# Two mixer gates' first 512 columns: from two plain row products to one seven-product Strassen unit spread over the gate columns and u, with a smaller scratch for dynamic DMAs and more buffers

## The chip, the cores and the metric

One core of a Trainium2 chip runs the whole program. Its engines are TensorE (PE, with PEld for its weight loads), VectorE (DVE), ScalarE (ACT), GpSimd (POOL) and SyncE (SP), which here only issues transfers. The metric is the device time of one execution in microseconds; the median of the runs is given. All data are float32, and a matmul in float32r is used three times over for one float32 product (below).

## The reference, cut to what matters

A trunk of two layers on 256 tokens of width 1024. Each layer is a half-step feed-forward (SwiGLU, 2816 wide), a mixer, and a second half-step feed-forward, each followed by a layer normalisation.

```python
z = x @ w_in
u, v, q, k, val, gates = jnp.split(z, SPLITS, axis=-1)
...
g = jax.nn.sigmoid(gates.reshape(bsz, seq, N_BRANCH, D_MODEL) + gate_b)
m = g[:, :, 0] * (h_a @ w_branch[0]) + g[:, :, 1] * (h_b @ w_branch[1])
return m @ w_out
```

`h_a` is a spatial gating unit (u times a causal mix of the normalised v), `h_b` is differential attention (q, k, val, 8 heads). There are two gates of 1024 columns each, one per branch. The change is in how the first 512 columns of both gates are computed.

## The kernel before

**Three matmuls for one.** A float32 operand is split into a high part (`hi`, rounded to float32r, by ACT) and a low part (`lo`, the difference, by DVE). A product is hi·hi + lo·hi + hi·lo. For each MB of weights that SP fetches into a `raw` buffer (4 of them), `stream` makes two half-blocks of 128 x 1024: ACT line 195 writes `whi`, DVE line 197 writes `wlo`. There are 8 buffers of each. Both can run ahead of TensorE as far as these buffers reach.

**Two forms of product.** In the row form (`rows_b`, `three`, line 283) the tokens are stationary and 512 weight columns move: per block of 128 tokens and 128 rows of weights, three matmuls of 512 columns. In the column form (`gemm_a2`, lines 295 and 302) the weights are stationary: 8 matmuls of 512 moving columns per 128 output columns, which carry the tokens' hi and lo parts side by side, and 8 of 256 for the low weights. Its results are emptied from PSUM by a copy of ACT (`r`, line 303) and an addition of DVE (line 305 or 307). `gemm_a2` takes 1 MB of weights for 256 output columns.

**Order of the work.** TensorE runs in the order in which the program is written. The instructions of the other engines are put in order by a planner ahead of time, by priority (`step` raises it per MB fetched) and by when their data are ready in the planner's own account; on the chip each engine then runs its list in that fixed order and waits where a datum is late. Tasks that go beside the products (attention, normalisation, sums) are generators: `beside(task, delay)` puts one on a list, and `beat(w)`, called after each product with its length, starts the next step of each task whose time has come. One beat is about 2.7 us of TensorE. `with behind(ins)` queues an instruction after another one on the same engine.

**The mixer.** val (row form, `gemm_b2`); eight query/key products in column form with rotary (`rope`); meanwhile four `attend` tasks, one for each pair of heads, run their steps: scores on TensorE (line 1017), maxima on DVE, exponentials on ACT (1031), the difference of the two maps (1040), POOL's copies that part the halves of a word for the transposing DMA (line 216, `parted`), the DMA on SP (`moved`, line 220), ACT's copies that join them again (1065), the products with val (1071 and 1073), and the norm per head, with POOL's small instructions (lines 268 to 276). Then for each gate in turn: `gate_rows`, the first 512 columns in row form (48 matmuls; two fetches), and `gate_columns`, the other 512 in two column products. After both gates, two column products of u, two row products of v, the other two of u, and the branches.

`gate_rows` is a plain product with all four half-blocks held (`tail=TAIL`): 2 token blocks x 8 row blocks x 3. DVE adds the bias row and ACT takes the tanh (lines 1125 and 1126). Its results, `grow[br][t]`, are read much later, by `branch_rows`.

**Strassen's scheme in the feed-forward part.** `seven` and `gemm_seven` already use Winograd's seven products for two 512-column weight groups at a time. The input is cut into token blocks t and row halves, the weights into row halves and two column groups. The sums of the input are made once (`sums_of_x`, `strassen_sums`: four differences on DVE, in place, and four splits into stationary blocks `xhs`). The sums of the weights are made either by DVE (`plus`) or by an accumulating DMA issued from POOL (`gather`, line 353), which adds a second block from HBM to a raw buffer: two issues of 512 KB. A block can be added to only when the split of its old value is done. `product` (line 376) is 4 row blocks x 3 matmuls of 512 columns into a bank that several products may share.

**Memory.** PSUM has two pools of four banks, `bank()` and `side_bank()`. In SBUF, beside the weight buffers, there are 26 `slot` tiles, and two pools of small tiles: `main` (`t512`, 3 tiles) and `side` (`s512`, 4 tiles). The normalisation leaves its transposed output in two tiles of each (`norm.rows`). [...]

Of the kernel before, what the change touches and what calls it, by code (L numbers as in the profile page):

```python
# [11 lines left out]
F32 = mybir.dt.float32  # L12
# [33 lines left out]
RAW, HL = 4, 8  # L46
# [8 lines left out]
def trunk(ctx, tc, x, xT, w13a, w13b, w2, wb, wqk, wu, wg, wgr, wbr, wbrr, wo, gateb, gatebr, sgug, sgub, sguwT, sgubias, lam, diffg,  # L55
# [42 lines left out]
    def t512(s, n=3):  # L98
        return tmp.tile([P, 512], F32, tag="main", name=name(s), bufs=n)

    def s512(s, n=4):
        return tmp.tile([P, 512], F32, tag="side", name=name(s), bufs=n)
# [491 lines left out]
    class Norm:  # L594
# [36 lines left out]
        def kept(self):  # L631

            y = self.y[-1][:, D - self.group :]
            unit, v = (tmp.tile([P, 512], F32R, tag="main", name=name("kept"), bufs=3) for _ in range(2))
# [145 lines left out]

    def ffn(l, f, i, norm, last=False):
# [57 lines left out]
        def sums_of_h():  # L839

            h11, h21, h12, h22 = (held[v] for v in ((0, 0), (0, 1), (1, 0), (1, 1)))
            made = [[h_hi[1], h_lo[1]]] + [[slots("sum", 2, F32R)[0] for _ in range(2)] for _ in range(2)]
            made.append([tmp.tile([P, 512], F32R, tag="side", name=name("sum"), bufs=4) for _ in range(2)])
            yield from strassen_sums(sums, made, h11, h21, h12, h22, 1.5)

        def sums_of_x():
# [6 lines left out]
            def home(tag):  # L853
                pool, n = {"main": (tmp, 3), "side": (tmp, 4), "slot": (act, 26)}[tag]
# [4 lines left out]

        def strassen_sums(to, made, v11, v21, v12, v22, apart=1, after=lambda: None):  # L860
            to[:] = [tuple(lambda k, v=v: v[:, k * P : (k + 1) * P] for v in m) for m in made]
            for n, (out, a, b, op) in ((0, (v22, v21, v22, ALU.subtract)), (2, (v21, v11, v21, ALU.subtract)),
                                       (1, (v11, v22, v11, ALU.subtract)), (3, (v12, v12, v11, ALU.add))):
                with behind(after()):
                    V.tensor_tensor(out=out, in0=a, in1=b, op=op)
                if n in (2, 3):
                    yield apart
            for n, out in ((0, v22), (2, v21), (1, v11), (3, v12)):
                split(*(v if len(out.shape) == 2 else v.rearrange("p (k t) -> p k t", k=4) for v in made[n]), out)
                yield apart  # L870
# [98 lines left out]
    def mixer(l, i, norm):  # L969
# [33 lines left out]
        def attend(hp, qT, kT):  # L1003
# [17 lines left out]
            def exps(t, banks):  # L1021
                nk = (t + 1) * P
                pp = []
                for m in range(2):
                    o = m * 4 + t * 2
                    p = s512("pp", 4)[:, : 2 * nk]
# [82 lines left out]

        for hp in range(HEADS // 2):  # L1110
# [6 lines left out]
        gates, grow = [], []  # L1117

        def gate_rows(br):

            gr = [slots("gr", 2)[0] for _ in range(NT)]
            grow.append(gr)

            def done(t, ps, c, n):
                added[0] = V.tensor_tensor(out=gr[t], in0=ps, in1=gbias[:, br * 512 : (br + 1) * 512], op=ALU.add).ins
                emptied[0] = A.activation(gr[t], gr[t], AF.Tanh, scale=0.5).ins
# [12 lines left out]
        for br in range(2):  # L1139
            gate_rows(br)  # L1140
            gate_columns(br)
# [43 lines left out]
        def spatial(gp):  # L1185
# [7 lines left out]
            s1 = s512("sgu", 4)  # L1193
# [164 lines left out]
```

## Time and profile before

| | before |
|---|---|
| runs, median of 3 | 1186.83 us (1186.79 to 1187.02) |
| profiled execution: first to last instruction (its span; the page has no other time of it) | 1185.1 us |
| instructions | 16676 |
| TensorE busy, matmuls | 1180.5 us, 5777 |
| DVE, ACT, POOL busy | 1013.1, 828.1, 287.5 us |
| DMA issued from SP (q1), from POOL (q0) | 248.67 MB, 24.71 MB |
| mixer of layer 0: query/key, gates and first half of u | 202.3 to 250.3 us, 250.3 to 312.9 us |
| the same of layer 1 | 788.8 to 836.6 us, 836.6 to 899.3 us |

A row of a group reads: line, engine, operation, tiles out<-in, shapes, count, then busy us and the mean of one in ns, then the idle time before them with what ended it. A row of a line's own view gives the shortest, middle and longest duration in ns. A row of the timeline is start, duration, engine, line, operation; in square brackets the idle time before it. A row of transfers gives count, KB each and the median us from issue to landing. Matmuls overlap, so the mean of one (390 ns) is longer than their spacing. PE is TensorE.

### The profile page before, as it was taken

To read this page: it belongs to the slowest core of one execution; us is meant where nothing else is said; L and a number is where in the kernel's file an instruction comes from. 1 tells how busy PE (TensorE), PEld (TensorE's weight loads), DVE (VectorE), ACT (ScalarE), POOL (GpSimd) and SP (SyncE) were. 2 spreads that over 40 slices of the span, in tenths; PEclk is the share of its full clock that TensorE was granted. 3 is DMA by queue.
4 is the path that set the end of the run, shared out by engine and by line. 5 is a ranking of instruction groups with operands and counts; after the bars stand their busy time and mean duration, and the time that the engine had idled before them with its cause. 6 is when DMAs were issued, how large, how long until landed. Compare 5 with 4: busy or idle time off the path is not lost.

```text
span 1185.1 us, 16676 instructions
## 1 busy us (share of the span) xinstructions
PE 1180.5 (100%) x5777; PEld 995.0 (84%) x5777; DVE 1013.1 (85%) x1562; ACT 828.1 (70%) x1419; POOL 287.5 (24%) x350
## 2 busy tenths in 40 slices
PE   9999999999999999999999999999999999999998
PEld 8888888888888888888888888888888888888887
DVE  6989989788688989889899889888965989988895
ACT  6688658559955677876667876576788556679761
POOL 1011201247420220051020161003564112102600
PEclk9999999999999999999999999999999999999999
DMA  9869976767865658699668689586666755786881
GB/s 355 265 198 262 287 273 208 266 193 238 246 205 173 227 188 273 187 275 267 239 220 265 190 278 280 198 290 232 212 204 208 250 181 174 247 254 208 273 260 36
DMA packets 129621, 275.10 MB, mean 232 GB/s; under 512 B 89041, under 2 KB 90369, under 8 KB 105473
## 3 DMA queue, kind: packets, MB, share of 16 engines
q1 hardware_dynamic: 121968, 248.67, 63.5%
q0 software_dynamic: 6992, 24.71, 8.7%
q8 instruction: 45, 0.74, 0.2%
q10 hardware_dynamic: 576, 0.66, 0.2%
q14 instruction: 40, 0.32, 0.1%
HBM read 248.05 MB, written 1.05 MB: 210 GB/s over the span
## 4 chain that ended last, share of the span: by engine, by line
PE 99%; DVE 0%; DVEq 0%; issue 0%
PE bank L283 46%; PE bank L295 15%; PE sbank L376 12%; PE bank L410 10%; PE bank L302 8%; PE sbank L410 3%; PE bank L530 2%; PE sbank L1017 1%; PE bank L376 1%; PE sbank L1073 1%; PE sbank L1191 1%; PE sbank L542 0%; PE sbank L1071 0%; PE sbank L714 0%; DVE xtok L701 0%; DVE st L643 0%
## 5 line engine op out<-in xcount | busy, mean ns | idle before, releaser
L197 DVE TENSOR_TENSOR wlo<-raw,whi 128x1024 fp32r<-128x1024 f32 (+1 forms) x346 | 379.4, 1123 | 51.8 <-ACT whi L195 38.0
L195 ACT ACTIVATE whi<-raw 128x1024 fp32r<-128x1024 f32 (+1 forms) x350 | 323.4, 952 | 135.1 <-PE bank L283 43.0
L283 PE MATMUL bank<-whi,x 128*128 128x512 f32 x1224 | 386.4, 390 | 0.0
L283 PEld LDWEIGHTS bank<-whi,x 128*128 128x128 f32 x1224 | 229.8, 188 | 47.8
L283 PE MATMUL bank<-wlo,x 128*128 128x512 f32 x612 | 238.2, 389 | 0.0
L249 DVE TENSOR_TENSOR wlo<-raw,whi 128x1024 fp32r<-128x1024 f32 (+1 forms) x123 | 142.9, 1185 | 20.3 <-ACT whi L247 11.4
L247 ACT ACTIVATE whi<-raw 128x1024 fp32r<-128x1024 f32 (+1 forms) x123 | 121.1, 1003 | 51.2 <-DVE raw L359 23.9
L295 PE MATMUL bank<-x,whi 128*128 128x512 f32 x640 | 153.3, 391 | 0.0
L295 PEld LDWEIGHTS bank<-x,whi 128*128 128x128 f32 x640 | 118.2, 188 | 23.8
L283 PEld LDWEIGHTS bank<-wlo,x 128*128 128x128 f32 x612 | 114.9, 188 | 23.1
L229 POOL COPY seven<-seven 128x512 uint16<-128x512 uint16 x16 | 58.8, 3733 | 135.2 <-ACT whi L195 54.6
L302 PEld LDWEIGHTS bank<-x,wlo 128*128 128x128 f32 x640 | 81.4, 191 | 2.9
L302 PE MATMUL bank<-x,wlo 128*128 128x256 f32 x640 | 82.6, 283 | 0.0
L410 PE MATMUL bank<-whi,hhi 128*128 128x512 f32 (+1 forms) x182 | 68.2, 374 | 0.0
L410 PE MATMUL bank<-whi,hlo 128*128 128x512 f32 (+1 forms) x182 | 67.9, 373 | 0.0
L410 PE MATMUL bank<-wlo,hhi 128*128 128x512 f32 (+1 forms) x182 | 67.9, 373 | 0.0
L993 POOL TENSOR_TENSOR swap<-swap,sin_t 128x512 f32<-128x512 f32 x16 | 26.9, 1680 | 101.2 <-DMA swap<-z 84.4
L757 POOL COPY nvia<-ntwo 128x256 uint16<-128x256 uint16 x20 | 10.0, 547 | 161.2 <-DMA ntwo<-nvia 148.2
L303 ACT ACTIVATE r<-bank 128x256 f32<-128x256 f32 x96 | 34.9, 373 | 16.3 <-PE bank L302 16.1
L376 PE MATMUL sbank<-whi,xhs 128*128 128x512 f32 x128 | 42.0, 389 | 0.0
L410 PEld LDWEIGHTS bank<-whi,hlo 128*128 128x128 f32 x182 | 34.3, 188 | 6.0
L410 PEld LDWEIGHTS bank<-whi,hhi 128*128 128x128 f32 x182 | 34.3, 188 | 6.0
(292 smaller groups left out, 2157.6 us busy)
## 6 DMA issues: line engine op xcount, KB each, us to landing
raw<-in_w13b SPq DMA_DIRECT2D x68, 1024.0 KB, 6.0
raw<-in_w SPq DMA_DIRECT2D x32, 1024.0 KB, 7.0
raw<-in_wb SPq DMA_DIRECT2D x16, 1024.0 KB, 6.7
raw<-in_wqk SPq DMA_DIRECT2D x16, 1024.0 KB, 6.2
home<-in_w13b SPq DMA_DIRECT2D x16, 512.0 KB, 5.9
raw<-in_w13a SPq DMA_DIRECT2D x8, 1024.0 KB, 4.9
home<-in_w SPq DMA_DIRECT2D x16, 512.0 KB, 4.9
raw<-in_wgr SPq DMA_DIRECT2D x8, 1024.0 KB, 5.4
```

The costliest lines, as they stand in the source:

```text
L195: inline(A, A.activation(h, r, AF.Copy).ins)
L197: low = eng.tensor_tensor(out=w, in0=r, in1=h.bitcast(F32), op=ALU.subtract).ins
L229: eng.tensor_copy(out=o, in_=i)
L247: a = A.activation(hi, src, AF.Copy).ins
L249: return a, eng.tensor_tensor(out=lo, in0=src, in1=hi.bitcast(F32), op=ALU.subtract).ins
L283: PE.matmul(ps, xx, w, start=start and n == 0, stop=stop and n == 2)
L295: PE.matmul(b[-1], hi[:, k * P : (k + 1) * P], xc(k), start=k == 0, stop=False)
L302: PE.matmul(b[n][:, :T], lo[:, k * P : (k + 1) * P], xc(k)[:, :T], start=False, stop=k == KT - 1)
L303: emptied[0] = A.activation(r[:, s], b[n][:, T:], AF.Copy, scale=scale).ins
L376: PE.matmul(ps, x[o](k), y, start=start and k == n == 0, stop=stop and k == 3 and n == 2, skip_group_check=True)
L410: PE.matmul(q[c][t][:, :n] if o == 0 else more[:, :n], x(k, t), y, start=k == 8 and m == 0 and (c, t) != (1, 0) and not o, stop=k == FT - ...
L993: turned_by[0] = G.tensor_tensor(out=s3, in0=s3, in1=s, op=ALU.mult).ins
```

## The change

In each mixer, `gate_rows` and its two plain products are gone. `gates_by_rows` computes the first 512 columns of both gates as one Strassen unit: the two gates are the two column groups, the two token blocks the two row groups. It is a generator with seven products; `next(products)` stands before each of the four gate-column products, before the first two products of u, and after the second. It fetches three blocks of weights (the first gate's two halves and the second gate's second), and adds to two of them four times by `gather`, one beat after the product that used the old value. The first bank is held through all seven products, another through the third and fourth. Sums go into the four tiles `g00` to `g11` in DVE additions; the four tanh are as before.

`sums_of_x` in the mixer starts 3.5 beats into the query/key products, with 0.7 beats between its steps, and takes eight `slot` tiles. `strassen_sums` is moved out of `ffn` unchanged, so that both can call it.

There are 5 raw buffers instead of 4, 4 `main` tiles instead of 3 and 5 `side` tiles instead of 4 (12 KB per partition more); the scratch for dynamic DMAs falls from 16384 to 4096 bytes per partition, 12 KB less.

```diff
-RAW, HL = 4, 8
+RAW, HL = 5, 8
+MAIN, SIDE = 4, 5
...
+        gates, grow, x_sums = [], [], []
+
+        def sums_of_x():
+            made = [slots("xhs", 4, F32R) for _ in range(4)]
+            t11, t12, t21, t22 = (norm.rows[v] for v in ((0, 0), (0, 1), (1, 0), (1, 1)))
+            yield from strassen_sums(x_sums, made, t11, t21, t12, t22, 0.7, lambda: added[0])
+
+        def gates_by_rows():
+
+            x11, x12, x22 = (tuple(lambda k, o=o, t=t, h=h: x_cat[h][:, k, o + t * P : o + (t + 1) * P] for o in (0, T))
+                             for t, h in ((0, 0), (0, 1), (1, 1)))
+            (w11, w21), (w12, w22) = ([wgr[l, br, 0][:, o : o + CH] for o in (0, CH)] for br in range(2))
+            grow.extend([slots("gr", 2)[0] for _ in range(NT)] for _ in range(2))
+            (g00, g10), (g01, g11) = grow
+
+            def add_in(raw, w):
+                def task():
+                    gather(raw, w)
+                    yield 0
+                beside(task(), 1)
+            bias = [gbias[:, br * 512 : (br + 1) * 512] for br in range(2)]
+
+            def sum_up(out, in0, in1, op, end=False):
+                added[0] = V.tensor_tensor(out=out, in0=in0, in1=in1, op=op).ins
+                if end:
+                    emptied[0] = A.activation(out, out, AF.Tanh, scale=0.5).ins
+
+            bx = bank()
+            r1 = fetch(w11)
+            product(bx, x11, pieces(r1), True, False)
+            add_in(r1, w12)
+            sum_up(g00, bx, bias[0], ALU.add)
+            yield
+            bq = bank()
+            product(bq, x12, pieces(fetch(w21)), True, True)
+            sum_up(g00, bq, g00, ALU.add, True)
+            yield
+            bz = bank()
+            product(bz, x_sums[0], pieces(r1), True, False)
+            add_in(r1, w22)
+            sum_up(g11, bz, bias[1], ALU.add)
+            yield
+            r3 = fetch(w22)
+            product(bz, x_sums[3], pieces(r3), False, True)
+            add_in(r3, w12)
+            sum_up(g01, bz, bias[1], ALU.add)
+            yield
+            product(bx, x_sums[1], pieces(r1), False, False)
+            add_in(r1, w21)
+            sum_up(g01, g01, bx, ALU.subtract, True)
+            yield
+            product(bx, x_sums[2], pieces(r3), False, False)
+            sum_up(g11, g11, bx, ALU.subtract, True)
+            yield
+            product(bx, x22, pieces(r1), False, True)
+            sum_up(g10, bx, bias[0], ALU.add, True)
+            yield
+
+        beside(sums_of_x(), 3.5)
...
-        gates, grow = [], []
-
-        def gate_rows(br):
...
-            gemm_b(wgr[l, br, 0], KT, xh, xl, done, tail=TAIL)
+        products = gates_by_rows()
 
         def gate_columns(br):
             gt = slots("gate", KT // 2)
             gates.append(gt)
             for c in range(KT // 4):
+                next(products)
                 (_, b), = gemm_a2([wg[l, br, c]], both, lambda m: t512("gz"), lambda: t512("r"))
...
         for br in range(2):
-            gate_rows(br)
             gate_columns(br)
...
             for gp in gps:
+                if gp < 2:
+                    next(products)
                 uu = slots("u", 2)[0]
...
+            if gp == 1:
+                next(products)
...
-    nc = bacc.Bacc("TRN2", target_bir_lowering=False, num_devices=1)
+    nc = bacc.Bacc("TRN2", target_bir_lowering=False, num_devices=1, dynamic_dma_scratch_size=4096)
```

More of the change, by code (lines that the diff above doesn't have):

```diff
@@ L96, in parts, with t512, s512 @@
         return (lambda k: f(k)[:, :T]), (lambda k: f(k)[:, T:])
[L98 to L102, printed above, removed]
+    def t512(s, dtype=F32):
+        return tmp.tile([P, 512], dtype, tag="main", name=name(s), bufs=MAIN)
+    def s512(s, dtype=F32):
+        return tmp.tile([P, 512], dtype, tag="side", name=name(s), bufs=SIDE)
     def sm(s, n, dtype=F32, bufs=2):
@@ L633, in kept @@
             y = self.y[-1][:, D - self.group :]
-            unit, v = (tmp.tile([P, 512], F32R, tag="main", name=name("kept"), bufs=3) for _ in range(2))
+            unit, v = (t512("kept", F32R) for _ in range(2))
             self.unit, hi, lo = unit[:, :P], v[:, : self.group], v[:, self.group :]
@@ L779, in close, with strassen_sums @@
             return self
+    def strassen_sums(to, made, v11, v21, v12, v22, apart=1, after=lambda: None):
+        to[:] = [tuple(lambda k, v=v: v[:, k * P : (k + 1) * P] for v in m) for m in made]
+        for n, (out, a, b, op) in ((0, (v22, v21, v22, ALU.subtract)), (2, (v21, v11, v21, ALU.subtract)),
+                                   (1, (v11, v22, v11, ALU.subtract)), (3, (v12, v12, v11, ALU.add))):
+            with behind(after()):
+                V.tensor_tensor(out=out, in0=a, in1=b, op=op)
+            if n in (2, 3):
+                yield apart
+        for n, out in ((0, v22), (2, v21), (1, v11), (3, v12)):
+            split(*(v if len(out.shape) == 2 else v.rearrange("p (k t) -> p k t", k=4) for v in made[n]), out)
+            yield apart
     def ffn(l, f, i, norm, last=False):
@@ L842, in sums_of_h @@
             made = [[h_hi[1], h_lo[1]]] + [[slots("sum", 2, F32R)[0] for _ in range(2)] for _ in range(2)]
-            made.append([tmp.tile([P, 512], F32R, tag="side", name=name("sum"), bufs=4) for _ in range(2)])
+            made.append([s512("sum", F32R) for _ in range(2)])
             yield from strassen_sums(sums, made, h11, h21, h12, h22, 1.5)
@@ L853, in home @@
             def home(tag):
-                pool, n = {"main": (tmp, 3), "side": (tmp, 4), "slot": (act, 26)}[tag]
+                pool, n = {"main": (tmp, MAIN), "side": (tmp, SIDE), "slot": (act, 26)}[tag]
                 return pool.tile([P, 512], F32R, tag=tag, name=name("xhs"), bufs=n)
@@ L858, in sums_of_x @@
             yield from strassen_sums(x_sums, made, t11, t21, t12, t22, after=lambda: None if norm else line[1])
[L860 to L870, printed above, removed]
         def seven(src, x_sums):
@@ L1025, in exps @@
                     o = m * 4 + t * 2
-                    p = s512("pp", 4)[:, : 2 * nk]
+                    p = s512("pp")[:, : 2 * nk]
                     for j in range(2):
@@ L1115, in mixer @@
                 gbias = bc_load(gatebr[l], qT[:, :1])
-        gates, grow = [], []
-        def gate_rows(br):
[L1121 to L1126, printed above, removed]
-            gemm_b(wgr[l, br, 0], KT, xh, xl, done, tail=TAIL)
+        products = gates_by_rows()
         def gate_columns(br):
```

2 lines of the change are left out of this document (1 added, 1 removed).

## The prediction, on record before the result

> **What bounds the kernel now.** I read the page first, then the chain of waits, the waits of TensorE, and after that the stretch that the change rewrites.
>
> ```profile
> span 1185.1 us, 16676 instructions
> PE 1180.5 (100%) x5777; PEld 995.0 (84%) x5777; DVE 1013.1 (85%) x1562; ACT 828.1 (70%) x1419; POOL 287.5 (24%) x350
> ...
> PEclk9999999999999999999999999999999999999999
> ...
> GB/s 355 265 198 262 287 273 208 266 193 238 246 205 173 227 188 273 187 275 267 239 220 265 190 278 280 198 290 232 212 204 208 250 181 174 247 254 208 273 260 36
> ...
> PE 99%; DVE 0%; DVEq 0%; issue 0%
> ```
> ```profile
> PE sbank L542 <- DVE warm L538: 1.0, 1, 1.0
> PE sbank L693 <- ACT minus L691: 0.2, 1, 0.2
> ```
>
> TensorE is the chain: 99% of it. Its granted clock is full in every slice, and the only two waits listed for it are 1.2 us in all, one before the first matmul and one in the last normalisation. So each matmul that disappears shortens the kernel by its spacing, as long as nothing new makes TensorE wait. What must be asked is whether the work beside it still arrives in time.
>
> The pieces of the chain, in order of time, give the spacing (start, us, line, count):
>
> ```profile
> 250.42 9.55 PE bank L283 x42
> ...
> 261.30 1.38 PE bank L283 x6
> 262.68 3.62 PE bank L295 x16
> 266.30 1.51 PE sbank L1017 x16
> 267.81 2.11 PE bank L302 x16
> 269.92 3.65 PE bank L295 x16
> 273.58 1.91 PE bank L302 x16
> ...
> 444.42 2.72 PE sbank L376 x12
> ```
>
> The 42 and 6 at L283 are the first gate's 48 row matmuls: 9.55 + 1.38 = 10.93 us, 0.228 each. Twelve matmuls of a Strassen product in the feed-forward part (L376) take 2.72 us, 0.227 each, although they too sit between other lines. A gate-column product is 16 + 16 matmuls, 3.65 + 1.91 = 5.56 us.
>
> **The sum.** Per layer the two gates have 2 x 48 = 96 row matmuls; seven block products of 4 row blocks with 3 matmuls have 84. Twelve fall away, 12 x 0.227 = 2.72 us, in two layers 5.44 us. The added matmuls have the same shapes, and no piece of the chain shows a cost at a change of line (1.91 us before and after), so interleaving is costed at nothing on TensorE.
>
> The profiled execution's own account is its span, 1185.1 us; the runs' median of 1186.83 lies 1.7 us above, and I carry that 1.7 over unchanged.
>
> **What is added beside TensorE**, per layer, with the rows for one instruction each:
>
> ```profile
> L249 DVE TENSOR_TENSOR wlo<-raw,whi 128x1024 fp32r<-128x1024 f32 x108 | 133.2, 1254 | 18.3 <-ACT whi L247 9.5 <-PE bank L302 6.9 <-issue 1.7
> L247 ACT ACTIVATE whi<-raw 128x1024 fp32r<-128x1024 f32 x108 | 112.1, 1055 | 48.2 <-DVE raw L359 23.9 <-PE bank L295 8.3 <-DVE wlo L249 4.8
> L865 DVE TENSOR_TENSOR held<-held,held 128x512 f32<-128x512 f32 x16 | 10.9, 684 | 0.0
> L249 DVE TENSOR_TENSOR sum<-held,sum 128x512 fp32r<-128x512 f32 x12 | 8.2, 684 | 0.0
> L247 ACT ACTIVATE hhi<-held 128x512 fp32r<-128x512 f32 x16 | 10.0, 624 | 0.2
> ```
> ```profile
> L1125 DVE TENSOR_TENSOR gr<-bank,bc x8: 677/684/692, 261.0 to 876.6; 128x512 f32<-128x512 f32 x8
> ```
>
> Sums of x, during the eight query/key products: 4 differences and 4 low halves on DVE, 8 x 0.684 = 5.5 us; 4 high halves on ACT, 4 x 0.624 = 2.5 us. Weights: seven products need 14 converted half-blocks where the old rows needed 8, so 6 more: 6 x 1.254 = 7.5 us of DVE and 6 x 1.055 = 6.3 us of ACT. Results: 7 additions instead of 4, 3 x 0.684 = 2.1 us of DVE; the four tanh stay. So DVE gets 5.5 us in the query/key stretch and 9.6 us in the gate stretch, ACT 2.5 and 6.3 us. The cover is this (query/key, gates with the first u, then v and the rest of u; last, two of layer 1):
>
> ```profile
> 202.30:250.30 48.00, 48.00 (x290) 41.82 (x289) 37.94 (x68) 25.66 (x49) 14.32 (x11) 1.00 0.71 241
> 250.30:312.90 62.60, 62.60 (x357) 53.95 (x357) 48.93 (x114) 56.39 (x148) 37.90 (x64) 1.00 0.77 233
> 312.90:347.20 34.30, 34.30 (x175) 29.25 (x174) 26.43 (x51) 24.71 (x48) 11.63 (x27) 1.00 0.67 220
> 788.80:836.60 47.80, 47.80 (x289) 41.62 (x288) 42.23 (x74) 26.95 (x50) 13.49 (x11) 1.00 0.72 251
> 836.60:899.30 62.70, 62.70 (x358) 54.03 (x357) 46.87 (x110) 56.15 (x148) 38.85 (x64) 1.00 0.70 224
> ```
>
> Columns: length, then TensorE, weight loads, DVE, ACT and POOL busy, clock, DMA share, GB/s. In the gate stretch ACT has 62.6 - 56.4 = 6.2 us free and would get 6.3 more while the stretch shrinks by 2.7: 62.7 us of work in 59.9. DVE: 48.9 + 9.6 = 58.5 in 59.9. Neither fits with ease; it goes only because conversions run ahead of TensorE:
>
> ```profile
> 301.07 1.05 ACT L195 ACTIVATE whi<-raw 128x1024 fp32r<-128x1024 f32 x1
> 302.15 1.23 DVE L197 TENSOR_TENSOR wlo<-raw,whi 128x1024 fp32r<-128x1024 f32 x1 [0.22 <-ACT whi L195]
> 313.08 6.83 PE bank L283 x30
> ```
>
> Counted in order, these two make the first half-block of v, which TensorE starts on at 312.9 (the chain dates a piece by the end of the one before): ready 10.8 us (ACT) and 9.5 us (DVE) early. ACT's lead falls by 6.3 + 2.7 = 9.0 us to 1.8 us if none of its idle time is put to use. DVE's falls by 9.6 + 2.7 = 12.3 us, to -2.8 us with no idle time used and to +4 us with half of its 13.7 us used. The third row of the table (7.9 us free on DVE, 9.6 on ACT) then rebuilds it. I take half: the lead holds on the whole, with single hand-overs late. The nearest such hand-over now is
>
> ```profile
> 258.46 0.82 ACT L1065 ACTIVATE d<-d 128x256 uint16<-128x256 uint16 x2
> 259.80 0.38 PE L1071 MATMUL sbank<-val,d 128*128 128x128 f32 x2
> ```
>
> 0.5 us between ACT's copy and the attention product that reads it. One more conversion of 1.05 us ahead of that copy makes it 0.5 us late. I charge one per layer, 1.0 us in all; from below it is 0 (the order of ACT is made anew), from above one set of rival 2 below.
>
> **PSUM.** One bank is held through all seven products, a second through the third and fourth. The gate columns then turn over two banks, not four. A bank's last matmul is followed by the other half's 16 / 2 low matmuls (0.96 us), the next product (2.72 us), and then its reuse: 3.7 us, against one copy and one addition of 256 columns, by the rows for 512 columns under 0.7 us each. Costed at nothing; it costs when ACT or DVE is over 2 us behind. **SBUF:** the normalisation's four transposed blocks are now held until the sums are made, some 20 us into the query/key stretch, out of the two pools that grow from 3 and 4 tiles to 4 and 5; there too a late sum would hold back the copies that empty PSUM, with the same slack.
>
> **Transfers.** Three fetches and four accumulating loads replace four fetches: 3 MB more per layer, 3.1 MB / 59.9 us = 53 GB/s on 233, 286 in all, below the 355 of the page's first slice.
>
> ```profile
> raw<-in_wgr SPq DMA_DIRECT2D x8, 1024.0 KB, 5.4
> ...
> home<-in_w POOLq DMA_DIRECT2D x8, 512.0 KB, 9.7
> ...
> raw<-in_w POOLq DMA_DIRECT2D x8, 512.0 KB, 7.5
> ...
> d<-aT SPq DMA_TRANSPOSE x8, 3.8
> ```
> ```profile
> L353 POOLq EVENT_SEMAPHORE  x25: 17/43/5441, 120.0 to 1129.1; - x25
> L353 POOL DMA_DIRECT2D raw<-in_w x8: 866/873/880, 137.9 to 1135.8; - x8
> ```
>
> An accumulated block is wanted again two products later, 2 x (2.72 + 5.56) = 16.6 us. It can start when the old block is converted, about 9 us before its use; two issues of 0.87 us and 9.7 us to landing, and 2 x 1.25 us of conversion: ready some 5 us after that use, 11 us to spare. Even a landing twice as long is covered. On SP the row fetches move to between the gate columns' and the first u's, in front of or behind the same transposes; three instead of four per layer, whose blocks land in 5.4 us and are wanted every 8.3 us: nothing. With two of the 5 weight buffers held, three are left for that beat.
>
> **POOL** gets 8 issues of 0.87 us, 7 us onto 37.9 of 62.6. Each waits for a conversion, and behind it stand the attention's copies:
>
> ```profile
> 263.80 2.73 POOL L216 COPY d<-d 128x256 uint16<-128x256 uint16 x2
> 277.76 1.42 ACT L1065 ACTIVATE aT<-d 128x512 uint16<-128x512 uint16 x2
> ```
> ```profile
> L229 POOL COPY seven<-seven x16: 1213/1730/15062, 106.9 to 1108.2; 128x512 uint16<-128x512 uint16 x16
> ```
>
> From POOL's copy (ends 266.5) to ACT's is 11.2 us, of which the transpose between takes 3.8 from issue to landing: 7 us of slack. The last row shows that POOL's copies stretch, from 1.2 to 15 us. [...]
>
> **The forecast:** -5.4 + 1.0 = -4.4: span 1180.7, time 1182.4. Its own range is 1181.2 to 1184.4.
>
> **Rivals.**
> 1. Everything stays covered: 1186.8 - 5.4 = 1181.4. For it: TensorE's idle time is nil now with DVE at 85%. Against: the 0.5 us hand-over.
> 2. DVE becomes the bound of the gate stretch. If no idle time there is put to use, the lead of 9.5 us ends at -2.8 in layer 0; in layer 1 DVE enters with less, because the query/key stretch has 5.6 us free for 5.5 (47.80 - 42.23), so I take another 1.5: -4.3. Together 7.1 us: 1188.5, inside the noise. Half of that gives 1185. For it: DVE's idle time is partly waits in a fixed order. Against: the row for low halves names ACT's conversion as what ended most of their idle time, and ACT is 10.8 us ahead.
> 3. POOL late, on the slower side: if a load waits for its conversion behind two such waits as long as the longest (2 x 5.4 us), the attention's copy is 10.9 - 7 = 3.9 us late at L1071, for two head pairs in two layers: 15.6 us, 1197. The kernel gets slower than measurement error once each is about 2 us late, that is, POOL over 9 us behind. Against it: conversions lead by about 9 us, and the issue follows later than they do.
> 4. The smaller scratch slows POOL's loads. No row shows its limit. If each added issue took twice its 0.87 us, POOL would have 2 x 7 = 14 us more per layer; with the 7 us of slack gone and 1 us late at two head pairs in two layers, 4 us: 1186.4. [...]
>
> **Chances.** Forecast 0.46, rival 1 0.23, rival 2 0.18, rival 3 0.09, rival 4 0.04. 0.2%, 2.4 us, is about what this kernel's measurement can tell from no change. Faster by more: the first two and a little of rival 2, 0.70; within: most of rival 2 and rival 4, 0.18; slower: rival 3 and the end of rival 2, 0.12. The range 1181.0 to 1188.0 takes in all but rival 3 and the end of rival 2.
>
> **What would show it.** Right: TensorE has 24 matmuls fewer and still no waits in the gate stretch beyond 1 us. Rival 2: idle TensorE before L295 or the new products, released by low halves of DVE. Rival 3: waits at L1071 and long POOL event waits at the accumulating load. Rival 4: longer issues there than 0.87 us, everywhere. A wait of the next product on a bank's emptying would make the PSUM step wrong; a wait of ACT on an accumulated block, the transfer step. Wrong altogether: no shorter span although the matmuls are gone.

## The result and the profile after

The changed kernel takes 1213.98 us (median of 4 runs, 1212.78 to 1217.55) against 1186.81 us for the kernel before beside it: a ratio of 1.0232, 95% interval 1.0216 to 1.0248. It is 27.2 us slower where the prediction had it 4.4 us faster.

The page of the changed kernel, its span, TensorE's busy time, the granted clock and the engines' shares of the chain:

```profile
span 1211.3 us, 16711 instructions
PE 1185.6 (98%) x5753; PEld 994.5 (82%) x5753; DVE 1042.6 (86%) x1596; ACT 839.6 (69%) x1439; POOL 301.1 (25%) x366
...
PEclk9999999999999999999999999999899999999999
...
PE 75%; DVE 8%; ACT 6%; POOL 4%; DMA 4%; issue 3%; SPq 0%; DVEq 0%; ACTq 0%; POOLq 0%
```

The 24 matmuls are gone (5777 to 5753), and the span is still 26.2 us longer. TensorE was 99% of the chain and is 75%. The list of what TensorE waited for (us in total, times, longest) has five lines that the list of before did not have:

```profile
PE bank L296 <- DVE z L306: 9.2, 3, 5.7
PE bank L284 <- ACT hb L1106: 6.1, 2, 3.0
PE bank L296 <- DVE gz L306: 3.6, 6, 1.0
PE bank L284 <- DVE hb L1108: 1.1, 2, 0.7
PE bank L284 <- DVE u L306: 1.0, 2, 0.8
```

These are 21.0 us. The lines of the changed kernel are one higher than before up to the mixers (L296 is the L295 of before). The first group and the third are the column products: the first matmul on a PSUM bank waits until VectorE's addition has emptied it, z being the result of a query/key column and gz that of a gate column. The u line is the same for the columns of u. The hb lines are the attention's result, which the mixer's output product reads. So 13.8 us are waits for a bank that was not yet empty (z, gz, u), and 7.2 us are waits for the attention.

The second part of the loss is the clock. Stretches of layer 0 (length, then TensorE, weight loads, VectorE, ScalarE and GpSimd busy, granted clock, DMA share, GB/s): the first wait on z, the 3.4 us that begin 0.7 us behind its end, the 3.4 us after those; the wait on hb, and the 3.4 us that begin 1.3 us behind its end. The last row is of layer 1, in the middle of its wait on z:

```profile
254.90:258.10 3.20, 0.20 (x1) 0.00 (x0) 2.27 (x11) 3.20 (x14) 2.06 (x1) 1.00 0.74 298
258.80:262.20 3.40, 3.40 (x12) 2.84 (x11) 3.31 (x9) 3.40 (x7) 0.00 (x0) 0.50 0.33 96
262.20:265.60 3.40, 3.40 (x29) 3.27 (x28) 2.79 (x4) 2.96 (x6) 3.31 (x4) 1.00 0.73 296
356.70:359.90 3.20, 0.16 (x1) 0.00 (x0) 3.20 (x9) 0.56 (x2) 0.00 (x0) 1.00 0.61 172
361.20:364.60 3.40, 3.28 (x8) 2.61 (x9) 2.69 (x6) 0.00 (x0) 0.00 (x0) 0.50 0.78 260
856.10:859.50 3.40, 0.50 (x1) 0.50 (x2) 3.06 (x8) 3.40 (x16) 1.00 (x1) 0.50 0.41 173
```

After these waits TensorE got half its clock, for 3.41 us from 258.79, 361.19 and 961.93 us and for 6.83 us from 856.12; its matmuls then start 0.43 us apart (860.02, 860.45), where the usual is 0.23. Over the run the mean granted clock is 0.993 (before: 1.000), so at most 0.007 x 1211.3 = 8.5 us are lost to it. Part of the half clock fell into layer 1's wait and cost nothing there: of the 17.1 us at half clock TensorE was busy in some 13.5, which makes 6.8 us. The account: 21.0 of new waits + 6.8 of clock - 5.4 of matmuls = 22.4 of the 26.2 us. The other 4 us are not assigned; the first two matmuls right behind a wait start 0.34 us apart (258.12 and 258.46, 359.90 and 360.24), not 0.23.

Why the first wait is there is seen when TensorE's and ScalarE's instructions are laid side by side (start, duration). TensorE in the changed kernel, the last query/key column's low products, then behind the first Strassen product the first gate column:

```profile
248.47 2.08 PE L303 MATMUL bank<-x,wlo 128*128 128x256 f32 x16
...
253.13 1.97 PE L296 MATMUL bank<-x,whi 128*128 128x512 f32 x8
258.12 2.40 PE L296 MATMUL bank<-x,whi 128*128 128x512 f32 x6 [3.02 <-DVE z L306]
```

ScalarE in the changed kernel, the first and last of head pair 1's eight exponentials, and the two copies (L304) that start to empty that query/key column's banks:

```profile
253.72 0.51 ACT L1032 ACTIVATE pp<-pp,mx 128x256 f32<-128x256 f32 x1 [7.55 <-DVE mx L1030]
...
256.86 0.39 ACT L1032 ACTIVATE pp<-pp,mx 128x128 f32<-128x128 f32 x1
...
257.25 0.36 ACT L304 ACTIVATE r<-bank 128x256 f32<-128x256 f32 x1
257.51 1.04 ACT L196 ACTIVATE whi<-raw 128x1024 fp32r<-128x1024 f32 x1
258.46 0.36 ACT L304 ACTIVATE r<-bank 128x256 f32<-128x256 f32 x1
```

TensorE is through with the banks at 250.4. ScalarE sat idle for 7.55 us, but the exponentials, which waited for VectorE's maxima, stand ahead of the copies in its fixed order. So the copies run at 257.25 and 258.46, and TensorE needs the bank at 254.9. And so it was before the change; ScalarE of the kernel before, same place:

```profile
252.19 0.51 ACT L1031 ACTIVATE pp<-pp,mx 128x256 f32<-128x256 f32 x1 [6.13 <-DVE mx L1029]
...
255.71 0.37 ACT L303 ACTIVATE r<-bank 128x256 f32<-128x256 f32 x1
...
256.93 0.37 ACT L303 ACTIVATE r<-bank 128x256 f32<-128x256 f32 x1
```

There too the copies came 5 to 7 us behind the matmuls, which ended at 250.4. It cost nothing because 10.9 us of row matmuls on two other banks followed; now 2.7 us follow.

One more thing differs in the transfers. Issues between 202 and 350 us or so (count, size, median us to landing), of before and then of after:

```profile
swap<-z SPq DMA_DIRECT2D x16, 128.0 KB, 2.1
...
d<-d SPq DMA_TRANSPOSE x4, 2.3
```
```profile
raw<-in_wgr POOLq DMA_DIRECT2D x8, 512.0 KB, 8.4
...
swap<-z SPq DMA_DIRECT2D x16, 128.0 KB, 4.1
...
d<-d SPq DMA_TRANSPOSE x4, 4.4
```

The rotation's swaps (swap) and the attention's transposes (d) take twice as long to land.

### The profile page after: what moved, and what is told of

Its sections match the earlier page's. It is cut to its first block, busy times and chain, and to the rows that moved or that the text cites. A ratio compares the mean times of both kernels' runs of the same rounds, so it can differ in the third digit from the quotient of the medians.

```text
span 1211.3 us, 16711 instructions
## 1 busy us (share of the span) xinstructions
PE 1185.6 (98%) x5753; PEld 994.5 (82%) x5753; DVE 1042.6 (86%) x1596; ACT 839.6 (69%) x1439; POOL 301.1 (25%) x366
## 4 chain that ended last, share of the span: by engine, by line
PE 75%; DVE 8%; ACT 6%; POOL 4%; DMA 4%; issue 3%; SPq 0%; DVEq 0%; ACTq 0%; POOLq 0%
PE bank L284 37%; PE sbank L377 12%; PE bank L411 9%; PE bank L296 6%; PE sbank L411 3%; PE bank L303 3%; DVE wlo L198 2%; DMA swap<-z 2%; PE bank L531 2%; ACT whi L196 1%; ACT pp L1032 1%; DMA raw<-in_wgr 1%; PE bank L377 1%; DVE wlo L250 1%; DMA on<-onT 1%
## 5 line engine op out<-in xcount | busy, mean ns | idle before, releaser
L198 DVE TENSOR_TENSOR wlo<-raw,whi 128x1024 fp32r<-128x1024 f32 (+1 forms) x330 | 358.7, 1114 | 50.2 <-ACT whi L196 42.8
L196 ACT ACTIVATE whi<-raw 128x1024 fp32r<-128x1024 f32 (+1 forms) x334 | 306.4, 946 | 108.0 <-PE bank L284 34.7
L284 PE MATMUL bank<-whi,x 128*128 128x512 f32 x1096 | 344.6, 389 | 0.0
L284 PEld LDWEIGHTS bank<-whi,x 128*128 128x128 f32 x1096 | 205.8, 188 | 42.6
L284 PE MATMUL bank<-wlo,x 128*128 128x512 f32 x548 | 213.2, 389 | 0.0
L250 DVE TENSOR_TENSOR wlo<-raw,whi 128x1024 fp32r<-128x1024 f32 (+1 forms) x151 | 179.8, 1212 | 29.8 <-ACT whi L248 22.8
L248 ACT ACTIVATE whi<-raw 128x1024 fp32r<-128x1024 f32 (+1 forms) x151 | 149.9, 1012 | 61.5 <-DVE raw L360 31.5
L296 PE MATMUL bank<-x,whi 128*128 128x512 f32 x640 | 157.8, 398 | 12.8 <-DVE z L306 9.2
L296 PEld LDWEIGHTS bank<-x,whi 128*128 128x128 f32 x640 | 119.6, 191 | 40.5 <-DVE z L306 10.2
L284 PEld LDWEIGHTS bank<-wlo,x 128*128 128x128 f32 x548 | 102.9, 188 | 21.3
L230 POOL COPY seven<-seven 128x512 uint16<-128x512 uint16 x16 | 67.0, 4248 | 125.1 <-ACT whi L196 81.1
L994 POOL TENSOR_TENSOR swap<-swap,sin_t 128x512 f32<-128x512 f32 x16 | 23.9, 1493 | 99.2 <-DMA swap<-z 90.3
L1032 ACT ACTIVATE pp<-pp,mx 128x256 f32<-128x256 f32 (+1 forms) x64 | 28.2, 442 | 23.4 <-DVE mx L1030 23.4
L304 ACT ACTIVATE r<-bank 128x256 f32<-128x256 f32 x96 | 33.9, 372 | 13.0 <-PE bank L303 12.7
```

Source lines behind the costliest of these rows:

```text
L196: inline(A, A.activation(h, r, AF.Copy).ins)
L198: low = eng.tensor_tensor(out=w, in0=r, in1=h.bitcast(F32), op=ALU.subtract).ins
L230: eng.tensor_copy(out=o, in_=i)
L248: a = A.activation(hi, src, AF.Copy).ins
L250: return a, eng.tensor_tensor(out=lo, in0=src, in1=hi.bitcast(F32), op=ALU.subtract).ins
L284: PE.matmul(ps, xx, w, start=start and n == 0, stop=stop and n == 2)
```

## The experiments

Four theories stood at the beginning, and the expectations name them by letter. D: VectorE is late because of the added sums of x. T: the small transfers are late because loads stand ahead of them. P: the gate columns have two banks where they had four. C: the added conversions make ScalarE and VectorE late. Theory S, formed after the first runs, is the sharper form of P: what makes the two banks too few is the softmax ahead of the copies in ScalarE's order. All ratios are against the kernel before on the same chip, with 95% intervals.

**Buffers and scratch alone** (e1_buffers), on the kernel before:

```diff
-RAW, HL = 4, 8
+RAW, HL = 5, 8
+MAIN, SIDE = 4, 5
...
+    nc = bacc.Bacc("TRN2", target_bir_lowering=False, num_devices=1, dynamic_dma_scratch_size=4096)
```

> The kernel before with only the buffer counts and the smaller scratch of the change (5 weight buffers instead of 4, the two shared pools 4 and 5 tiles instead of 3 and 4, scratch of 4096); the gates stay as they were. Theory T (small transfers come late because weight loads stand ahead of them): a fifth weight buffer lets loads go ahead of the query/key transfers; the swap transfers take about 4 us to landing instead of 2.1 and the time rises by 3 to 10 us over 1186.8. Theory D (VectorE comes late because of the added sums) and theory P (two PSUM banks instead of four for the gate columns): 1186.8 within 1 us, swap transfers at 2.1 us.

Measured: 1186.97 us, ratio 1.0001 (0.9992 to 1.0010). The swaps did come later, as T had it:

```profile
DMA to landing us min/median/max: 1.9/3.3/5.8
```

That cost nothing. So neither the scratch nor the added buffers are the cause by themselves, and a swap that is 1 us later in the median is still covered.

**Without the sums, without the loads, without both** (e2_no_sums, e3_no_accum, e5_neither):

```diff
-        beside(sums_of_x(), 3.5)
...
+        x_sums[:] = [x22, x21, x12, x11]     # e2 and e5: blocks of x instead
...
             def add_in(raw, w):
-                def task():
-                    gather(raw, w)
-                    yield 0
-                beside(task(), 1)
+                pass                         # e3 and e5
```

> The changed kernel without the sums of x: the products that read them read blocks of x itself, so the gates' first 512 columns are not what the reference has. Leaves 8 VectorE and 4 ScalarE operations per layer out of the query/key stretch, everything else as changed. Theory D: the waits at the end of the query/key stretch (3.2 and 5.9 us, and the half clock behind them) go, and most of the later ones with them: 1190 to 1196. Theory T: those waits stay in the main, 1207 to 1214.

> The changed kernel without the accumulating loads: the buffers are converted again with their old contents, so the gates' first 512 columns are not what the reference has. Leaves 4 MB of transfers per layer and GpSimd's 8 issues with their waits out. Theory T: swap transfers back near 2.1 us, the transposes near 4 us, time 1190 to 1198. Theory D: the waits at the end of the query/key stretch stay, 1207 to 1214.

> The changed kernel without the sums of x and without the accumulating loads (both as in the two runs beside it; the gates' first 512 columns are not what the reference has). What is left of the change: 84 matmuls instead of 96, the products between gate columns, 6 more conversions, PSUM banks held, more buffers. Theory P: only the three short waits per layer at gate columns are left, 4.5 us in all, 1181.4 + 4.5 = 1186. If conversions or buffers are to blame: above 1190. If nothing of P is left either: 1181 to 1182.

Measured: 1208.27 us without the sums (1.0185, 1.0169 to 1.0201), 1206.68 without the loads (1.0172, 1.0156 to 1.0187), 1203.29 without both (1.0135, 1.0118 to 1.0152). Sums and loads are worth 5.7 and 7.3 us, together 10.7. The run without the sums lies in T's band, that without the loads just below D's, so each run speaks against the theory that it was to bear out. With both gone the kernel is still 16.6 us slower than before, and 22 us above what its matmuls would give. The waits of e5_neither:

```profile
PE bank L284 <- ACT hb L1106: 6.1, 2, 3.0
PE bank L296 <- DVE gz L306: 3.9, 4, 1.5
PE bank L296 <- DVE z L306: 1.9, 1, 1.9
PE bank L284 <- DVE u L306: 1.2, 2, 0.6
```

These are the same places as in the whole change. The larger part of the loss is thus in what this run keeps: the products between the columns with the banks that they hold, and the six added conversions. By the band set beforehand (above 1190) it speaks for conversions or buffers; e1 has cleared the buffers, and theory C stays open until f9 below. P named the place and was far off in size: it had 4.5 us, without the waits on hb and without the clock.

**Beginning the attention earlier** (f6_neither_early without sums and loads, f5_after_early whole):

```diff
-            beside(attend(hp, qT, kT), 4.5 + 2.1 * hp)
+            beside(attend(hp, qT, kT), (4.5, 5.9, 7.9, 9.9)[hp])
```

> The kernel without the sums of x and without the accumulating loads (the gates' first 512 columns are not what the reference has), with one thing more: the attention of head pairs 1 to 3 begins 0.7 to 0.9 beats earlier, so that their scores come before a column's matmuls and not in the middle of them, and ScalarE has the softmax's exponentials done before that column's banks are to be emptied. Theory S (a bank's emptying stands behind 3.5 us of exponentials in ScalarE's order, and with a product of 2.7 us between the columns TensorE is back at the bank before it is empty): the waits on z and gz (5.8 us) go with the half clock behind the first (1.7), and what is late after them comes back in part: 1186 to 1195. Theory C (the six added conversions per layer are what makes ScalarE and VectorE late): the waits stay or move, above 1200.

> The changed kernel whole, with the attention of head pairs 1 to 3 begun 0.7 to 0.9 beats earlier (before a column's matmuls and not in the middle of them). Theory S: of 27 us lost, the waits on z and gz (13 us) and the half clock behind two of them (5 us) go in the main: 1196 to 1203. Theory T (small transfers stand behind the loads) and D (VectorE late by the sums): the attention is late all the same, 1206 to 1214.

Measured: 1193.60 us (1.0058, 1.0043 to 1.0073), 9.7 less than without the edit, and 1207.38 us (1.0186, 1.0168 to 1.0204), 6.6 less. In both the waits on hb are gone entirely: the attention was late at the mixer's output, and no longer is. The wait on z did not go, against the expectation, but grew, as these rows of f6_neither_early show (1.9 in e5), and the third of f5_after_early (9.2 in the whole change):

```profile
PE bank L296 <- DVE z L306: 3.6, 2, 3.5
PE bank L296 <- DVE gz L306: 3.4, 2, 1.7
...
PE bank L296 <- DVE z L306: 12.6, 3, 7.9
```

So f6 lies in S's band by luck: the time came from the attention, and not from the waits that S named. f5 missed that band and lies in that of T and D. C would have kept f6 above 1200, so f6 speaks against it.

Why the wait on z stayed is seen in VectorE of f6_neither_early:

```profile
246.26 0.74 DVE L308 SCALAR_TENSOR_TENSOR z<-bank,r 128x256 f32<-128x256 f32 x2
250.10 0.69 DVE L998 TENSOR_TENSOR qk<-qk,swap 128x512 f32<-128x512 f32 x1 [3.10 <-POOL swap L994]
250.71 0.41 DVE L1030 CUSTOM_DVE_ANT_0 pp<-sbank,mask 128x256 f32<-128x256 f32 x1
```

The scores came earlier, but the maxima (L1030) stand in VectorE's order behind the rotation's addition, which waits for a swap and GpSimd's product with it. So the exponentials still began at 251.2, ahead of the copies, which ran at 256.6 and 257.0.

**The products in pairs** (f3_neither_pairs without sums and loads, f4_after_pairs whole):

```diff
+        def turns(n):
+            for _ in range(n):
+                next(products)
...
             for c in range(KT // 4):
-                next(products)
+                turns(*((2, 2), (2, 1))[br][c:c + 1])
...
-                if gp < 2:
-                    next(products)
...
-            if gp == 1:
-                next(products)
```

> The kernel without the sums of x and without the accumulating loads (the gates' first 512 columns are not what the reference has), with the products in pairs: two before the first gate column, two before the second, two before the third, one before the fourth, none at u. Between a column's last matmul and the next use of its banks lie 5.4 us and not 2.7. Theory S: the first wait shrinks to 1 us at most and that at the second and third column goes; the fourth keeps its own; 1192 to 1199. Theory C: no better than 1202, for the conversions come in pairs too.

> The changed kernel whole, with the products in pairs (two before each of the first three gate columns, one before the fourth). Theory S alone: about 1202. But an accumulated block is now wanted 8.3 us after its first use and not 16.6, and its load took 6 to 12 us to landing: ScalarE and VectorE wait for it, new waits at the third and fifth product; 1205 to 1215.

Measured: 1206.27 us (1.0163, 1.0148 to 1.0178) and 1227.33 us (1.0343, 1.0324 to 1.0362), both worse than without the edit: f3 lies above S's 1192 to 1199, f4 above its 1205 to 1215. In f3_neither_pairs the wait on z shrank to 0.6 us and that on gz went, as S said; in f4 6.5 us on z were left. In their place TensorE of f3 waited twice, up to 7.0 us, before the fourth product:

```profile
PE bank L377 <- DVE bc L591: 12.6, 2, 7.0
```

The third and fourth product share a bank, and VectorE's addition that reads it between them ran only at 274.83, behind seven low halves and eight maxima. A column's 5.56 us used to lie there. In f4_after_pairs the same addition cost 12.7 us in the two layers, and the second product's addition another 2.7; ScalarE waited 10.3 us for accumulated blocks, as expected. The pairs settle nothing on C; they show a second reader of PSUM that comes late by its engine's order.

**The copies ahead of the exponentials** (f8_after_late1 whole, f9_neither_late1 without sums and loads): as the early attention, but pair 1 begins behind the last query/key column.

```diff
-            beside(attend(hp, qT, kT), 4.5 + 2.1 * hp)
+            beside(attend(hp, qT, kT), (4.5, 7.8, 7.9, 9.9)[hp])
```

> The changed kernel whole, with the attention of head pair 1 begun behind the last query/key column's matmuls and copies (1.2 beats later than in the change), that of pairs 2 and 3 0.8 and 0.9 beats earlier. In ScalarE's order the two copies that empty that column's banks now stand ahead of pair 1's exponentials. Theory S: the waits on z at the first gate column (4.6 and 7.9 us with the early attention, 8.5 us of half clock behind them) go: 1186 to 1191. Theory D or T: something else keeps the column's banks full, the waits stay: 1200 to 1208.

> As the run beside it, without the sums of x and without the accumulating loads (the gates' first 512 columns are not what the reference has). Theory S: the wait on z (3.6 us, 1.7 of half clock behind it) goes, that at the third gate column (1.7 us per layer) stays: 1185 to 1188. The difference to the run beside it is what sums and loads cost once the softmax is out of the way.

Measured: 1200.55 us (1.0119, 1.0104 to 1.0134) and 1190.09 us (1.0031, 1.0019 to 1.0042). ScalarE of f9_neither_late1, with a copy at the bank's last matmul and 7 us ahead of the exponentials:

```profile
248.43 0.38 ACT L304 ACTIVATE r<-bank 128x256 f32<-128x256 f32 x1 [0.57 <-PE bank L303]
...
255.61 0.51 ACT L1032 ACTIVATE pp<-pp,mx 128x256 f32<-128x256 f32 x1 [4.83 <-DVE mx L1030]
```

The wait on z at the first gate column is gone in both, and with it S is shown for this wait; f9 differs from f6 in nothing but the beginning of pair 1, and is 3.5 us faster. f9 also keeps all six conversions per layer and lies 8.7 us above what its matmuls would give, where e5 lay 22 above: in this order C can be at most that. But a new wait came, the scores of pair 2 behind ScalarE's copy of pair 0's result, which empties one of the attention's own banks. The waits of f8_after_late1:

```profile
PE sbank L1018 <- ACT on L1077: 7.7, 2, 4.7
PE bank L296 <- DVE z L306: 3.4, 2, 2.0
```

The z here are two waits inside layer 1's query/key stretch. f8 missed its 1186 to 1191 by this new wait, by those two, and by the half clock (at most 0.006 x 1198.8 = 7.2 us). f9 missed its 1185 to 1188 by the same new wait, 2.8 us, and the half clock behind it.

**Sums and loads one at a time in this order** (g1_late1_no_sums, g2_late1_no_accum): f8 with the edits of e2 and of e3.

> The kernel with head pair 1's attention behind the last query/key column (pairs 2 and 3 earlier), without the sums of x (the gates' first 512 columns are not what the reference has); the accumulating loads stay. Theory T (loads ahead of the small transfers): most of the 10.5 us stay, 1197 to 1200. Theory D (VectorE's added work): most of them go, 1190 to 1194.

> The same order without the accumulating loads (the gates' first 512 columns are not what the reference has); the sums of x stay. Theory T: most of the 10.5 us go, 1190 to 1194, the last swaps land in 2 to 4 us again. Theory D: 1197 to 1200.

Measured: 1194.75 us (1.0069, 1.0054 to 1.0084) and 1195.27 us (1.0073, 1.0056 to 1.0090). The sums are worth 5.8 us, the loads 5.3; both together were 10.5. So each is about half, in this order as in the first; both runs lie between the two bands, and neither D nor T alone explains the rest. The waits in layer 1's query/key stretch are gone without the sums (no line for z) and halved without the loads:

```profile
PE sbank L1018 <- ACT on L1077: 5.9, 2, 3.2
PE bank L296 <- DVE z L306: 1.7, 2, 1.2
```

**The loads later, the sums earlier** (g3_late12_loads, g7_sums_early), both whole:

```diff
-            beside(attend(hp, qT, kT), 4.5 + 2.1 * hp)
+            beside(attend(hp, qT, kT), (4.5, 7.8, 10.1, 9.9)[hp])
...
                 def task():
-                    gather(raw, w)
+                    with behind(turned_by[0]):
+                        gather(raw, w)
...
-        beside(sums_of_x(), 3.5)
+        beside(sums_of_x(), 1.5)             # g7 alone
```

> The changed kernel whole, pair 1's attention behind the last query/key column, pair 2's behind the second gate column, pair 3's before the fourth, and each accumulating load issued after GpSimd's last product for the rotation, so that none stands ahead of a swap. Theory T: the waits in the query/key stretch of layer 1 (3.5 us) go, the scores wait less for their bank: 1190 to 1195. Theory D: no change there, 1198 to 1202; at the later head pairs the loads still stand ahead of transposes in either case.

> As the run beside it, with the sums of x begun 2 beats (5.5 us) earlier, nearer the start of the query/key stretch. Theory D: the work that is ahead of the late rotations of pair 1 moves away from them, 2 to 4 us less than the run beside it. Theory T: the same within 1.5 us.

Measured: 1214.67 us (1.0255, 1.0217 to 1.0293) and 1213.70 us (1.0227, 1.0212 to 1.0243): a clear miss, as slow as the change itself. The waits on z went but for 0.5 us, those on gz came to 22.7 us in g3. ScalarE of g3_late12_loads:

```profile
259.17 0.19 ACT L1079 ACTIVATE s<-sums 128x4 f32<-128x4 f32 x1
268.55 1.06 ACT L248 ACTIVATE whi<-raw 128x1024 fp32r<-128x1024 f32 x1 [9.20 <-DMA raw<-in_wgr]
269.51 0.37 ACT L304 ACTIVATE r<-bank 128x256 f32<-128x256 f32 x1
```

Now it is a conversion that stands ahead of the copy and waits 9.2 us for its accumulated block. It is the same fault with another culprit: whatever ScalarE waits for, the banks wait too. What the loads' place alone is worth can't be read from this run. Begun earlier, the sums changed 1.0 us, within what these runs scatter; D's 2 to 4 us did not come.

**Pair 2's scores half a column later** (h1_after_order whole, h2_neither_order without sums and loads): f8 and f9 with `(4.5, 7.8, 8.4, 9.9)`.

> The changed kernel whole, pair 1's attention behind the last query/key column as in f8, pair 2's scores half a gate column later than in f8 (between the second column's two halves). If the scores' wait for their bank comes from the moved attention alone: it shrinks by 1.8 us in each layer, the half clock behind it (6.8 us) goes in the main, 1191 to 1196 after 1200.6. If pair 2's exponentials now stand ahead of the second column's copies: a wait on gz of 1 to 2 us per layer in its place, 1196 to 1201.

> The same order without the sums of x and without the accumulating loads (the gates' first 512 columns are not what the reference has). If nothing else is left of the loss: the scores' wait (2.8 us) and the half clock behind it (1.7) go, 1185 to 1187 after 1190.1, still 4 to 5 us above the 1181.4 of the matmuls alone only if the gate columns' waits stay.

Measured: 1207.65 us (1.0174, 1.0157 to 1.0191) and 1191.90 us (1.0052, 1.0035 to 1.0069), both slower than f8 and f9 and outside every band that was set. The scores' wait is gone from both; h2's list has in its place

```profile
PE bank L296 <- DVE gz L306: 6.3, 3, 2.3
```

and h1's 9.2 us on gz, up to 4.4, with 4.7 us before an attention product. So the wait had only moved. In each order tried, some reader of a bank stood behind something else. No kernel here beats the kernel before; the fastest that does the whole change is f8, 1.2% slower.

**A wait of known size** (c1_clock2, c2_clock8), on the kernel before: GpSimd copies a tile two or eight times, and the first column matmul of each feed-forward part comes behind one matmul on the copy.

```diff
+    stall = [None]
+
+    def late(src, n):
+        for _ in range(n):
+            v = small.tile([P, T], F32R, tag="late", name=name("late"), bufs=2)
+            G.tensor_copy(out=v, in_=src)
+            src = v.bitcast(F32)
+        stall[0] = v[:, :P]
...
+                if (n, t) == (NB - 1, 1):
+                    late(s[:, :T], 2)        # 8 in c2
...
                 b.append(bank())
+                if stall[0]:
+                    v, stall[0] = stall[0], None
+                    PE.matmul(b[-1][:, :P], v, v, start=True, stop=True)
```

> The kernel before with a delay of known size at four places (scratch of 4096 to make room): before the first column matmul of each feed-forward part TensorE does one matmul on a tile that GpSimd has copied twice in a row, starting when the row matmuls before it are through, so that TensorE waits some 1.5 to 2 us each time. Only if a wait of more than about 3 us costs clock: the time rises by the waits themselves, 6 to 8 us, and the granted clock stays full. If every wait costs clock: 1.7 us more for each, 13 to 15 us.

> The same with eight copies by GpSimd in a row, so that TensorE waits some 5 to 7 us at the four places. If a wait of more than about 3 us costs clock: half clock for 3.4 us or twice that behind each wait, the time rises by the waits (20 to 28 us) and 1.7 or 3.4 us more for each: 28 to 42 us in all. If not: by the waits alone.

Measured: 1204.92 us (1.0152, 1.0131 to 1.0172) with waits of 3.8 us and three times 2.4, 11.2 in all, and 1220.74 us (1.0285, 1.0264 to 1.0306) with 23.9 us. That is 18.2 and 34.0 us more, 7 and 10 beyond the waits themselves. Stretches of c1_clock2: the first wait, the stretch behind it, the last wait, the stretch behind that:

```profile
112.00:116.10 4.10, 0.27 (x3) 0.03 (x1) 3.76 (x5) 2.30 (x4) 2.15 (x3) 1.00 1.00 153
116.10:119.50 3.40, 3.40 (x9) 2.72 (x10) 0.00 (x0) 0.00 (x0) 2.64 (x4) 0.51 0.92 206
...
1125.30:1128.00 2.70, 0.26 (x3) 0.03 (x1) 2.09 (x3) 1.78 (x3) 1.55 (x3) 1.00 0.96 328
1128.00:1131.50 3.50, 3.50 (x16) 2.93 (x17) 0.18 (x1) 1.06 (x1) 0.81 (x2) 1.00 1.20 243
```

Three of the four waits were followed by half clock, three times 1.7 us lost, which is about what the run's mean clock of 0.996 lacks (0.004 x 1203.8 = 4.8); the last was not, though it was as long as two of the others. The waits had come out longer than meant, and the limit of 3 us in the expectation was too high. On top of its own length a wait cost 1.7 us in the mean here (7.0 / 4) and 2.5 in c2 (10.1 / 4).

## Why the prediction was wrong, step by step

- **TensorE's saving** (12 x 0.227 us a layer): right. The 24 matmuls are gone, and the products keep their 2.72 us.
- **PSUM** ("3.7 us, against one copy and one addition of 256 columns, by the rows for 512 columns under 0.7 us each. Costed at nothing"): this step failed. It priced the emptying of a bank by the length of the two instructions, when what counts is when they run. The copies came 5 to 7 us behind the matmuls in the kernel before already, and a look at ScalarE's order around 250 us would have shown it. The time to the next use fell from over 10 us to 4.5. In the changed kernel 13.8 us of the waits are of this kind. e5, f8 and f9 carry this: with sums and loads out such waits stay, and with the copies put ahead of the exponentials the longest of them is gone.
- **The hand-over** at the attention's product (0.5 us): it never waited in the changed kernel. The 1.0 us charged there was put in the wrong place; the attention came late at its other end, hb, which the prediction doesn't name. It cost 6.1 + 1.1 us of waits, which are gone in f5 and f6, where the attention begins earlier. Why it came late is argued only: the products give one beat less in the order of the work, and TensorE's own waits put the attention's steps later still. Added work of POOL is not needed for it, since e5 has none of the added issues and the same 6.1 us.
- **Sums beside TensorE** (5.5 us of VectorE in a stretch with 10.1 free in layer 0): VectorE's busy time rose from 37.94 in 48.0 us to 42.35 in 47.7, by 4.4 us; the eight operations are there, and three others fell outside the stretch:

```profile
202.60:250.30 47.70, 47.70 (x288) 41.53 (x287) 42.35 (x73) 27.30 (x52) 14.48 (x13) 1.00 0.74 232
```

  They were hidden from TensorE there, but they were not free: 5.7 and 5.8 us in e2 and g1. That they cost this by making VectorE late for the attention is argued. Free time was taken for slack, though part of it was waiting in a fixed order. Rival 2 said as much and stopped at 1188.5, since it counted VectorE's lead on the weights alone.
- **Transfers** (landing 9.7 us, wanted after 16.6): right for the loads themselves in the changed kernel, which landed after 8.4 us in the median; ScalarE waited 0.2 us for them. In other orders the slack was gone (16.3 us of such waits in g3). What they delay was not costed: the swaps and transposes beside them (2.1 to 4.1 us, 2.3 to 4.4 us; the buffers alone made the swaps 3.3). With the loads out the time fell by 7.3 us in e3 and 5.3 in g2. That the slower small transfers are the way by which loads cost time is likely from these rows, and argued rather than shown.
- **POOL** (rival 3): TensorE has no wait at the attention's product, so this rival fell. The issues took 0.88 us in the median, as costed.
- **Scratch** (rival 4): fell by e1, 1.0001.
- **The clock**: not in the prediction at all, some 7 us. Its sum had a wait cost its own length.
- **The range**: each single term was bounded, but the terms were taken as independent of each other. The rivals were each one late engine, where the loss was one late copy that made the next things late.

## What to carry to other kernels

A PSUM bank was free here when its reader had run, not when its reader could run (matmuls through at 250.4, copies at 257.25 and 258.46): before a product is put between two uses of a bank, read in the trace at what time the copies and additions ran and what stood ahead of them on their engine. With TensorE 99% of the chain, the gain of fewer matmuls was small and certain here (5.4 us), and what they gave cover to was neither (21.0 us of new waits); look for every wait that their time was hiding. Of the waits that stand above with the clock behind them, of 1.9 us (e5_neither) to 5.7 us (the changed kernel), all but one of 2.4 us (c1_clock2) ended in half clock or were followed by it; such a wait is to be priced with it.

## What the runs showed of the chip

In the changed kernel the half clock began on one grid. In its records of the granted clock the slow stretches are 3.41 us long or twice that, but for one that the end of the run cuts off, and they begin at 258.8, 361.2, 856.1 and 961.9 us: 30, 145 and 31 times 3.413 us apart. When this grid is laid over the run's matmul starts (the steps of over 0.5 us between them, less the usual 0.23, summed for each 3.413 us), five of its windows had TensorE idle for 2.7 to 3.2 us, one of them itself at half clock, and each was followed by half clock; four at full clock had 0.6 to 1.1 us, and none was. What lies between, this run does not show. In e5_neither a wait of 1.9 us was enough (the wait, and a stretch that begins 1.5 us behind it),

```profile
254.80:256.90 2.10, 0.19 (x1) 0.00 (x0) 1.34 (x3) 2.10 (x10) 0.00 (x0) 1.00 0.70 297
258.40:261.80 3.40, 3.40 (x15) 3.18 (x14) 3.37 (x8) 3.40 (x7) 0.47 (x1) 0.50 0.52 118
```

and the last of 2.4 us in c1_clock2 was not. Where a wait lies on the grid may be the reason, an estimate that takes the spacing of 3.413 us from the changed kernel: counted back from 258.4, a window of e5_neither reaches from 255.0 to 258.4 and holds nearly all of its wait; counted on from the half clock at 116.1, a border falls at about 1126.4 in c1_clock2, inside its last wait (the row 1125.30:1128.00 above). No run here varies the place of a wait alone.
